# S5 tables of a hybrid diffusion step: transposing the factors of the matrix to the state, or their product

## The chip, the core and the metric

The kernel runs on one core of a Trainium2 chip. The metric is the device time of one execution in microseconds (us), the median of three runs. PE is TensorE (the matrix engine), PEld its weight loads, DVE is VectorE, ACT is ScalarE, POOL is GpSimd and SP is SyncE; the last two also issue DMAs, each on a queue of its own. Engines take their instructions in a fixed order each and wait for one another by semaphores. Lines (L138) are lines of the kernel before, except in the orders of the changed kernel, which have its own.

## The reference

One inference step of a backbone of two layers with shared weights, for 128 context tokens and 256 latent ones, of 1024 channels. A layer is a half-step SwiGLU FFN, a mixer of three branches (S5 scan, convolution, chunk MLP) and another half FFN. Only the S5 branch is touched. For each of 32 groups of 16 channels, two directions and 64 states:

```python
mag = jnp.exp(a_re * dt)
abar_r, abar_i = mag * jnp.cos(a_im * dt), mag * jnp.sin(a_im * dt)
...
bbar_r = qr[..., None] * b_re - qi[..., None] * b_im
bbar_i = qr[..., None] * b_im + qi[..., None] * b_re
bu_r = jnp.einsum('gph,blgh->blgp', bbar_r, u)
...
_, _, sr, si = lax.associative_scan(_ssm_combine, (ar, ai, bu_r, bu_i), reverse=reverse, axis=1)
y = jnp.einsum('ghp,blgp->blgh', c_re, sr) - jnp.einsum('ghp,blgp->blgh', c_im, si)
```

`abar` is the step of the state, `bbar` the factors of the input (`u` is a part of a projection), and `c` the factors of the output.

## The kernel before

**Weights.** The program is one long list of products of weights with all 384 tokens. A unit of weights (up to 512 rows by 256 columns, 128x1024 on the chip) is loaded by SP into `wr`, split by ACT into a rounded half `wh` (L126) and by DVE into the rest `wl` (L105), and used in 24 matmuls of 384 columns (L198, L199, L200, `mm3`): rounded weight by rounded input `hh` (or `ah`), by the input's rest `hl` (`al`), and rest of the weight by rounded input. `wr`, `wh` and `wl` have three buffers each, and units are asked for two ahead (`LOOK`), so the split of one waits until the matmuls of an earlier one have freed its buffers. PE's order is the one in which the code is written; the scheduler of the framework sets the order on the other engines, which follows that of writing with some interleaving.

**Tracks.** Other work is written as generators ("tracks") that go forward a little after each unit (`tick`): the modulation vectors (`modev`, L138, and `modw`, L385, on the bank `ax`) and the S5 tables (`tables`, at a rate of 1.9 steps a unit in layer 0 and 1.6 in layer 1). Where a track has PE work, this stands in PE's order between two units.

**S5 parameters.** The S5 scan is done in chunks of TC = 8 steps. `s5_params` (L776), once for both layers, works out `pw`, the powers 0 to 8 of `abar` with the state (two directions by 64) on the 128 partitions, and writes them in two orders, `w` = 0 and 1, through `px` to DRAM (`px_d`).

**S5 tables.** `s5_tables` (L912), once a layer, reads both back (`pxl`: `psx` and `pyx`) and then takes the 32 groups of channels in four "groups" of GB = 8. Each begins with two transposes of the output factors `cr` on PE into a bank `tb`, copied by ACT to `cT` (L946); the input factors `bb`, four products `cm` and two sums on DVE (L105) from `braw`; their shifted copy `bp`, four ACT copies of 64 partitions (L956, L957), both `bb` and `bp` zeroed on POOL first; and `nci` (L118). Then follow two sub-blocks of GS = 4, each with

- `my`, the matrix from the state to the outputs: powers `pyx` by `cT`, six DVE operations of 512 elements a partition, stored on POOL's queue (L993);
- `mt`, the matrix to the state: powers `psx` by `bb`, six such DVE operations (L105), with the state on the partitions;
- the responses within a chunk: 32 small matmuls of `bp`, `bb` with `my`, `cT`, `nci` (L1012, L1022), copied to `kall`;
- eight transposes of `mt` on PE (L138) into two banks, two ACT copies to `ms` (L1038), which has steps and channels on the partitions, and its store (L1039).

At the end of a group twelve small stores of `kall` to `kd` (L1042 to L1044), eight loads of `mib` (L1047), each onto 16 partitions, and the store of `mi` go by POOL's queue. In the mixer `load_to` (L1132) reads `ms` on SP's queue and PE multiplies it with `U`. Of temporaries, pool `c4` has five buffers (`my`, `mt`, `ms`, `mib`), `c2` seven (`pxl`, `bb`, `bp`, `tp`), `s1` seven (`cT`, `cm`, `braw`, `cr`, `kall`, `nci`), and of banks `tb` there are two.

Of the kernel before, what the change touches and what calls it, by code (L numbers as in the profile page):

```python
# [19 lines left out]
P = 128  # L20
DEPTH = 2
# [35 lines left out]
def hybrid_step(ctx: ExitStack, tc: tile.TileContext, I, pos_r, pos_c, y_prompt, y_sample, new_state):  # L57
# [649 lines left out]
    px_d = [drm.tile([P, 2, 2, TC, G], F32, tag=f"px{l}", name=f"px{l}") for l in range(DEPTH)]  # L707
# [68 lines left out]
    def s5_params(raw, ldt):  # L776
# [81 lines left out]
        lo_i = slice(TC - 1, None, -1), slice(1, TC + 1)  # L858
        hi_i = slice(0, TC), slice(TC, 0, -1)
        for w in range(2):  # L860
            px = c4([P, DEPTH, 2, TC, G], "px")
            for i in range(2):
                for rows, ix in ((LO, lo_i[w]), (HI, hi_i[w])):
                    src = pw[rows, i, ix, :].rearrange("p n (l g) -> p l n g", l=DEPTH)
                    for l in range(DEPTH):
                        act.activation(px[rows, l, i], src[:, l], AF.Copy)
            for l in range(DEPTH):
                q.dma_start(px_d[l][:, w], px[:, l])
# [43 lines left out]
    def s5_tables(l):  # L912
        q = nc.gpsimd
        px = []
        for w in range(2):
            t = c2([P, 2, TC, G], "pxl")
            q.dma_start(t, px_d[l][:, w])
            px.append(t)
        psx, pyx = px
# [18 lines left out]
        for gb in range(G // GB):  # L938
# [20 lines left out]
            ts_(nci, cT[:, 1], -1.0)  # L959
            if gb + 1 < G // GB:  # L960
                nxt = load_bc(gb + 1)
            kall = s1([P, 2, 9 * H], "kall")
            for sb in range(GB // GS):
                s0 = sb * GS

                def pexp(tab, i):
                    v = tab[:, i, :, g0 + s0 : g0 + s0 + GS]
                    return v.rearrange("p n g -> p g n").unsqueeze(3).to_broadcast(sh)
# [5 lines left out]
                b_r, b_i = vec(bb[:, 0]), vec(bb[:, 1])  # L974
                my = c4([P, GS, 2, TC, H], "my")
                t1, t2 = c2(sh, "tp1"), c2(sh, "tp2")
                mul(t1, pexp(pyx, 0), c_r)
                mul(t2, pexp(pyx, 1), c_i)
# [3 lines left out]
                mul(t1, pexp(pyx, 1), c_r)  # L982
                yield
                mul(t2, pexp(pyx, 0), c_i)
# [10 lines left out]
                mt = c4([P, GS, 2, TC, H], "mt")  # L995
                t1, t2 = c2(sh, "tp1"), c2(sh, "tp2")
                mul(t1, pexp(psx, 0), b_r)
                mul(t2, pexp(psx, 1), b_i)
                yield
                sub(mt[:, :, 0], t1, t2)  # L1000
                t1, t2 = c2(sh, "tp1"), c2(sh, "tp2")
# [839 lines left out]
```

## Time and profile before

| | |
|---|---|
| median of 3 runs | 1785.54 us (1782.42 to 1787.46) |
| the profiled execution | 1785.44 us, span 1783.6 us |
| busy in the span | PE 1758.1, PEld 1672.6, DVE 1247.1, ACT 795.0, POOL 202.8 us |
| tables of layer 0 | first `cr` transposes at 161.91 us, second at 207.83 us |
| DMA | 344.37 MB, mean 193 GB/s |

The profile is of one execution, by the hardware profiler. The span runs from its first instruction to its last. Register, branch, semaphore and DMA-issuing instructions are not counted as busy, matmuls overlap in time (the start of the next is the better measure of one), and a row with xN stands for N instructions in a row. "[2.37 <-DMA kd]" in a row means that the engine was idle for 2.37 us just before it and what ended that.

### The profile page before, as it was taken

What the parts mean: (1) busy time and instruction counts of PE and PEld (TensorE: products, weight loads), DVE (VectorE), ACT (ScalarE), POOL (GpSimd) and SP (SyncE); (2) the same over time, 40 slices, a digit from 0 to 9 for tenths busy, and PEclk for the clock granted to TensorE, in tenths of its full rate; (3) what the DMA queues carried; (4) which work ended last, traced back from release to release, by engine and by line L of the source; (5) the groups of instructions that cost most, each with busy time, mean ns of one, the idle gap of its engine ahead of it and who ended that gap; (6) DMA issues with size and microseconds to landing.
All of it is one profiled execution on the core that took longest, in us unless ns stands there. A gap on an engine that the chain in (4) does not pass through costs nothing.

```text
span 1783.6 us, 29079 instructions
## 1 busy us (share of the span) xinstructions
PE 1758.1 (99%) x11186; PEld 1672.6 (94%) x11186; DVE 1247.1 (70%) x2344; ACT 795.0 (45%) x1330; POOL 202.8 (11%) x400
## 2 busy tenths in 40 slices
PE   6999999999999999999999999999999999999997
PEld 4899999999999989999999899999999999999997
DVE  4496676778987776679387666777799677544435
ACT  3344333564455553233357233336744546433233
POOL 2012343310010000000001133232100000000000
PEclk9999999999999999999999999999999999999999
DMA  9768788765744567788346776667666343443332
GB/s 329 258 220 272 231 255 268 225 194 185 243 144 128 168 223 225 253 276 257 118 130 206 231 225 214 177 198 226 174 209 182 119 131 119 130 130 123 126 124 77
DMA packets 253746, 344.37 MB, mean 193 GB/s; under 512 B 22399, under 2 KB 216651, under 8 KB 253608
## 3 DMA queue, kind: packets, MB, share of 16 engines
q1 hardware_dynamic: 228504, 299.18, 52.9%
q0 software_dynamic: 17088, 39.51, 7.3%
q10 hardware_dynamic: 8016, 3.82, 0.8%
q8 instruction: 88, 1.44, 0.3%
q14 instruction: 50, 0.41, 0.1%
HBM read 309.75 MB, written 32.70 MB: 192 GB/s over the span
## 4 chain that ended last, share of the span: by engine, by line
PE 97%; DVE 1%; DMA 1%; ACT 1%; issue 0%; DVEq 0%; ACTq 0%
PE mm L198 30%; PE mm L199 29%; PE mm L200 29%; PE ax L385 3%; PE tb L1159 1%; PE tb L138 1%; PE tb L1237 1%; DMA wr<-in_w_in_dram 1%; PE tb L1012 0%; PE ax L503 0%; PE ax L138 0%; DMA crow<-in_c_dram 0%; DVE sqacc L105 0%; PE mm L1528 0%; PE ax L489 0%; PE mm L1530 0%
## 5 line engine op out<-in xcount | busy, mean ns | idle before, releaser
L105 DVE TENSOR_TENSOR wl<-wr,wh 128x1024 fp32r<-128x1024 f32 (+2 forms) x389 | 457.4, 1176 | 355.5 <-ACT wh L126 350.2
L126 ACT ACTIVATE wh<-wr 128x1024 fp32r<-128x1024 f32 (+1 forms) x387 | 395.6, 1023 | 646.4 <-PE mm L199 483.9
L198 PE MATMUL mm<-hh,wh 128*128 128x384 f32 x1840 | 628.5, 342 | 3.9 <-ACT hh L609 3.9
L199 PE MATMUL mm<-hl,wh 128*128 128x384 f32 x1840 | 616.9, 335 | 0.7 <-DVE hl L105 0.7
L200 PE MATMUL mm<-hh,wl 128*128 128x384 f32 x1840 | 616.8, 335 | 0.0
L198 PEld LDWEIGHTS mm<-hh,wh 128*128 128x128 f32 x1840 | 346.2, 188 | 33.4 <-issue 18.4
L199 PEld LDWEIGHTS mm<-hl,wh 128*128 128x128 f32 x1840 | 346.3, 188 | 1.7 <-DVE hl L105 1.5
L200 PEld LDWEIGHTS mm<-hh,wl 128*128 128x128 f32 x1840 | 346.0, 188 | 0.1
L198 PE MATMUL mm<-ah,wh 128*128 128x384 f32 x800 | 271.9, 340 | 0.0
L199 PE MATMUL mm<-al,wh 128*128 128x384 f32 x800 | 269.8, 337 | 0.0
L200 PE MATMUL mm<-ah,wl 128*128 128x384 f32 x800 | 269.4, 337 | 0.0
L198 PEld LDWEIGHTS mm<-ah,wh 128*128 128x128 f32 x800 | 150.2, 188 | 9.6 <-issue 6.7
L199 PEld LDWEIGHTS mm<-al,wh 128*128 128x128 f32 x800 | 150.3, 188 | 0.0
L200 PEld LDWEIGHTS mm<-ah,wl 128*128 128x128 f32 x800 | 150.2, 188 | 0.0
L123 DVE SCALAR_TENSOR_TENSOR x<-mm,gt,x 128x128 f32<-128x128 f32 x224 | 83.1, 411 | 33.2 <-PE mm L200 32.8
L198 PE MATMUL mm<-xh,wh 128*128 128x386 f32 x240 | 84.8, 353 | 0.0
L200 PE MATMUL mm<-xh,wl 128*128 128x386 f32 x240 | 82.0, 342 | 0.0
L199 PE MATMUL mm<-xl,wh 128*128 128x386 f32 x240 | 82.0, 342 | 0.0
L126 ACT ACTIVATE ah<-av 128x384 fp32r<-128x384 f32 x82 | 42.1, 519 | 87.8 <-DVE av L105 87.5
L123 DVE SCALAR_TENSOR_TENSOR macc<-modw,silu_c,macc 128x1024 f32<-128x1024 f32 x56 | 69.9, 1279 | 10.3 <-DMA modw<-in_w_mod_dram 10.3
L123 DVE SCALAR_TENSOR_TENSOR cacc<-pad,pv,cacc 128x399 f32<-128x399 f32 x120 | 68.6, 629 | 0.0
L385 PE MATMUL ax<-modw,silu_c 128*32 128x512 f32 (+1 forms) x576 | 62.5, 516 | 0.0
(316 smaller groups left out, 1868.0 us busy)
## 6 DMA issues: line engine op xcount, KB each, us to landing
wr<-in_ffn_w_dram SPq DMA_DIRECT2D x256, 512.0 KB, 3.6
modw<-in_w_mod_dram SPq DMA_DIRECT2D x144, 512.0 KB, 5.1
wr<-in_w_gate_dram SPq DMA_DIRECT2D x48, 512.0 KB, 4.7
wr<-in_w_in_dram SPq DMA_DIRECT2D x24, 512.0 KB, 3.9
my<-my POOLq DMA_DIRECT2D x16, 512.0 KB, 5.8
ms<-ms POOLq DMA_DIRECT2D x16, 512.0 KB, 5.2
m_ms<-ms SPq DMA_DIRECT2D x16, 512.0 KB, 5.5
m_my<-my SPq DMA_DIRECT2D x16, 512.0 KB, 9.9
```

The source lines that it names most:

```text
L105: (eng or dve).tensor_tensor(out, a, b, op=op)
L123: dve.scalar_tensor_tensor(out, a, s, b, op0=op0, op1=op1)
L126: act.activation(hi, full, AF.Copy)
L138: pe.transpose(out, in_, ident[:rows, :rows])
L198: pe.matmul(out, wh[:, k, cols], xh, start=first, stop=False)
L199: pe.matmul(out, wh[:, k, cols], xl, start=False, stop=False)
L200: pe.matmul(out, wl[:, k, cols], xh, start=False, stop=last)
L385: pe.matmul(b[32 * s : 32 * s + 32, :w], silu_c[:, k, :], raws[i][:, c : c + w], start=(k == 0), stop=(k == KD - 1), skip_group_check=True,)
L1159: pe.matmul(b[:, g * NCH : (g + 1) * NCH], d["ms"][g // GS][:, g % GS, i, :], U[:, q * GB + g, :], start=True, stop=True,)
L1237: pe.matmul(b[64 * half : 64 * half + NCH, g * P : (g + 1) * P], u, w, start=(n == 0), stop=(n == 2), skip_group_check=True,)
```

## The change

The matrix to the state is no longer formed with the state on the partitions and transposed. `s5_params` writes the powers in one order to `px_d` (half of it before), transposes `pw` itself with eight transposes, rearranges it with four ACT copies into `pws`, and writes it to DRAM (`pt_d`: real and imaginary, step, channel group, state). Each group copies its `bb` on ACT to `bc`, transposes this on PE right behind `cr`, copies the result to `bts` and writes that to DRAM (`bt_d`). For each sub-block `to_rows_in` loads both in 16 transfers of 16 partitions on POOL's queue, eight of `pt` (L1029 of the changed kernel, each powers of one step given to 16 partitions) and eight of `bt` (L1030), and `to_rows` forms `ms` by six DVE operations of 128x512, with steps and channels on the partitions. The generator of a group yields in a new order: `my` of both sub-blocks early, the second sub-block's loads behind the first one's `ms`.

```diff
-    px_d = [drm.tile([P, 2, 2, TC, G], F32, tag=f"px{l}", name=f"px{l}") for l in range(DEPTH)]
+    px_d = [drm.tile([P, 2, TC, G], F32, tag=f"px{l}", name=f"px{l}") for l in range(DEPTH)]
+    pt_d = [drm.tile([2, TC, G, P], F32, tag=f"pt{l}", name=f"pt{l}") for l in range(DEPTH)]
+    bt_d = [drm.tile([H, G, 2, P], F32, tag=f"bt{l}", name=f"bt{l}") for l in range(DEPTH)]
...
-        lo_i = slice(TC - 1, None, -1), slice(1, TC + 1)
-        hi_i = slice(0, TC), slice(TC, 0, -1)
-        for w in range(2):
-            px = c4([P, DEPTH, 2, TC, G], "px")
-            for i in range(2):
-                for rows, ix in ((LO, lo_i[w]), (HI, hi_i[w])):
-                    src = pw[rows, i, ix, :].rearrange("p n (l g) -> p l n g", l=DEPTH)
-                    for l in range(DEPTH):
-                        act.activation(px[rows, l, i], src[:, l], AF.Copy)
+        px = c4([P, DEPTH, 2, TC, G], "px")
+        for i in range(2):
+            for rows, ix in ((LO, slice(1, TC + 1)), (HI, slice(TC, 0, -1))):
+                src = pw[rows, i, ix, :].rearrange("p n (l g) -> p l n g", l=DEPTH)
+                for l in range(DEPTH):
+                    act.activation(px[rows, l, i], src[:, l], AF.Copy)
+        for l in range(DEPTH):
+            q.dma_start(px_d[l], px[:, l])
+        yield
+
+        pws = c4([P, TC, P], "pws")
+        for i in range(2):
+            b = tb_bank()
+            for m in range(TC // 2):
+                transpose(
+                    b[:, m * P : (m + 1) * P], pw[:, i, 2 * m : 2 * m + 2, :].rearrange("p n r -> p (n r)"), P
+                )
+            bv = b.rearrange("p (m s) -> p m s", s=P)
+            o = pws[:, 4 * i : 4 * i + 4]
+            act.activation(o[:, ::-1, LO], bv[:, :, LO], AF.Copy)
+            act.activation(o[:, :, HI], bv[:, :, HI], AF.Copy)
+            yield
+        for n2 in range(2):
             for l in range(DEPTH):
-                q.dma_start(px_d[l][:, w], px[:, l])
+                r = n2 * NG + l * G
+                rows_d = pt_d[l].rearrange("i j g s -> (i j) g s")
+                for half, off in ((LO, 1 - n2), (HI, n2)):
+                    q.dma_start(
+                        rows_d[off::2, :, half].rearrange("m g s -> g m s"), pws[r : r + G, :, half]
+                    )
...
-        px = []
-        for w in range(2):
-            t = c2([P, 2, TC, G], "pxl")
-            q.dma_start(t, px_d[l][:, w])
-            px.append(t)
-        psx, pyx = px
+        pyx = c2([P, 2, TC, G], "pxl")
+        q.dma_start(pyx, px_d[l])
...
             nci = s1([P, GB, H], "nci")
             ts_(nci, cT[:, 1], -1.0)
+            bc = s1([P, 2, GB, H], "bc")
+            act.activation(bc, bb[:, :, :, :H], AF.Copy)
+            b = tb_bank()
+            for i in range(2):
+                transpose(b[:, i * P : (i + 1) * P], bc[:, i].rearrange("p g h -> p (g h)"), P)
+            bts = s1([P, 2, P], "bts")
+            act.activation(bts.rearrange("p i s -> p (i s)"), b[:, : 2 * P], AF.Copy)
+            q.dma_start(bt_d[l][:, gs].rearrange("h g i s -> g h (i s)"), bts.rearrange("r i s -> r (i s)"))
             if gb + 1 < G // GB:
                 nxt = load_bc(gb + 1)
             kall = s1([P, 2, 9 * H], "kall")
-            for sb in range(GB // GS):
+
+            def from_rows(sb):
...
-                mt = c4([P, GS, 2, TC, H], "mt")
-                t1, t2 = c2(sh, "tp1"), c2(sh, "tp2")
-                mul(t1, pexp(psx, 0), b_r)
-                mul(t2, pexp(psx, 1), b_i)
+
+            def to_rows_in(sb):
+                gr = slice(g0 + sb * GS, g0 + (sb + 1) * GS)
+                pt = c4([P, 2, GS, P], "pt")
+                bt = c4([P, GS, 2, P], "bt")
+                for j in range(TC):
+                    rows = slice(j * H, (j + 1) * H)
+                    src = pt_d[l][:, j, gr]
+                    q.dma_start(pt[rows], src.unsqueeze(0).to_broadcast([H, 2, GS, P]))
+                    q.dma_start(bt[rows], bt_d[l][:, gr])
+                ins.append((pt, bt))
+
+            def to_rows(sb):
+                pt, bt = ins[sb]
+                ms = c4([P, GS, 2, P], "ms")
+                t1, t2 = (c2([P, GS, P], f"tp{i}") for i in (1, 2))
+                mul(t1, pt[:, 0], bt[:, :, 0])
+                mul(t2, pt[:, 1], bt[:, :, 1])
                 yield
-                sub(mt[:, :, 0], t1, t2)
-                t1, t2 = c2(sh, "tp1"), c2(sh, "tp2")
-                mul(t1, pexp(psx, 0), b_i)
+                sub(ms[:, :, 0], t1, t2)
+                t1, t2 = (c2([P, GS, P], f"tp{i}") for i in (1, 2))
+                mul(t1, pt[:, 0], bt[:, :, 1])
                 yield
-                mul(t2, pexp(psx, 1), b_r)
-                add(mt[:, :, 1], t1, t2)
-                for _ in range(3):
-                    yield
+                mul(t2, pt[:, 1], bt[:, :, 0])
+                add(ms[:, :, 1], t1, t2)
+                q.dma_start(ms_d[l][:, g0 + sb * GS : g0 + (sb + 1) * GS], ms)
+                yield
+
+            def responses(sb):
+                s0 = sb * GS
+                my = mys[sb]
                 b = tb_bank()
 
                 for i in range(2):
@@ -1028,15 +1072,19 @@
                             skip_group_check=True,
                         )
                 act.activation(kall[:, sb, :], b[:, : 9 * H], AF.Copy)
-                ms = c4([P, GS, 2, P], "ms")
-                for g2 in range(0, GS, 2):
-                    b = tb_bank()
-                    for j in range(4):
-                        transpose(
-                            b[:, j * P : (j + 1) * P], mt[:, g2 + j // 2, j % 2].rearrange("p i h -> p (i h)"), P
-                        )
-                    act.activation(ms[:, g2 : g2 + 2].rearrange("p g r c -> p (g r c)"), b, AF.Copy)
-                q.dma_start(ms_d[l][:, g0 + s0 : g0 + s0 + GS], ms)
+
+            mys, ins = [], []
+            yield from from_rows(0)
+            to_rows_in(0)
+            yield from from_rows(1)
+            responses(0)
+            yield from to_rows(0)
+            to_rows_in(1)
+            yield
+            yield
+            responses(1)
+            yield
+            yield from to_rows(1)
```

What this does to the orders, at the last change of group in layer 0 (from the third to the fourth group).

PE, at the transposes of `cr` between two units of the first FFN or the mixer, before (`hh`, `hl` the inputs of the matmuls, `tb` a bank):

```order
L198 MATMUL mm<-hh_527,wh 128x384
L199 MATMUL mm<-hl_528,wh 128x384
L200 MATMUL mm<-hh_527,wl 128x384
L138 MATMUL tb<-ident,cr 128x128 x2
L198 MATMUL mm<-hh_345,wh 128x384
L199 MATMUL mm<-hl_346,wh 128x384
L200 MATMUL mm<-hh_345,wl 128x384
```

and in the changed kernel:

```order
L198 MATMUL mm<-hh_531,wh 128x384
L199 MATMUL mm<-hl_532,wh 128x384
L200 MATMUL mm<-hh_531,wl 128x384
L138 MATMUL tb<-ident,cr 128x128 x2
L138 MATMUL tb<-ident,bc 128x128 x2
L198 MATMUL mm<-hh_349,wh 128x384
L199 MATMUL mm<-hl_350,wh 128x384
```

The two transposes of `bc` stand directly behind those of `cr`, with no matmul of weights between them.

DVE, before, at the input factors `bb` of the fourth group (`cm` are the products, `wl` splits of weights):

```order
L105 TENSOR_TENSOR al<-av,ah 128x384
L105 TENSOR_TENSOR wl<-wr,wh 128x1024
L105 TENSOR_TENSOR cm_3360<-q_t,braw 128x128
L105 TENSOR_TENSOR cm_3361<-q_t,braw 128x128
L105 TENSOR_TENSOR cm_3365<-q_t,braw 128x128
L105 TENSOR_TENSOR bb<-cm_3360,cm_3361 128x8x16
L105 TENSOR_TENSOR cm_3366<-q_t,braw 128x128
L105 TENSOR_TENSOR wl<-wr,wh 128x1024
L105 TENSOR_TENSOR bb<-cm_3365,cm_3366 128x8x16
L118 TENSOR_SCALAR nci<-cT 128x128
L105 TENSOR_TENSOR tp_3380<-pxl,cT 128x512
L105 TENSOR_TENSOR tp_3381<-pxl,cT 128x512
```

and in the changed kernel, the operations just ahead of the same two sums `bb` (`tp`, `ms` are of the third group, both sub-blocks):

```order
L105 TENSOR_TENSOR tp_3159<-pt,bt 128x512
L105 TENSOR_TENSOR ms<-tp_3154,tp_3155 128x4x128
L105 TENSOR_TENSOR tp_3160<-pt,bt 128x512
L105 TENSOR_TENSOR ms<-tp_3159,tp_3160 128x4x128
L105 TENSOR_TENSOR tp_3306<-pt,bt 128x512
L105 TENSOR_TENSOR tp_3307<-pt,bt 128x512
L105 TENSOR_TENSOR tp_3311<-pt,bt 128x512
L105 TENSOR_TENSOR ms<-tp_3306,tp_3307 128x4x128
L105 TENSOR_TENSOR tp_3312<-pt,bt 128x512
L105 TENSOR_TENSOR ms<-tp_3311,tp_3312 128x4x128
L105 TENSOR_TENSOR bb<-cm_3428,cm_3429 128x8x16
L105 TENSOR_TENSOR bb<-cm_3433,cm_3434 128x8x16
```

The sums `bb` stand behind the twelve operations on `pt` and `bt` of the group in hand, and behind `nci` of the fourth group there is no weight split between them.

POOL, in the changed kernel, around the store of the first `ms` of the third group (`kd` are the small stores of `kall`):

```order
L1019 DMA my_130<-my 128x1024
L1090 DMA kd_132<-kall 16x2x112
L1091 DMA kd_132<-kall 16x2x112
L1092 DMA kd_132<-kall 16x2x16
L1090 DMA kd_132<-kall 16x2x112
L1029 DMA pt<-pt_142 16x2x512
L1046 DMA ms_128<-ms 128x1024
L1030 DMA bt<-bt_144 16x1024
L1029 DMA pt<-pt_142 16x2x512
L1030 DMA bt<-bt_144 16x1024
L1029 DMA pt<-pt_142 16x2x512
L1030 DMA bt<-bt_144 16x1024
```

One load of `pt` of the second sub-block stands ahead of the store of `ms`, and fifteen of the sixteen behind it.

## Rows read from the trace of the kernel before

**Rows 1.** The page, busy times (part 1) and the chain (part 4).

```profile
PE 1758.1 (99%) x11186; PEld 1672.6 (94%) x11186; DVE 1247.1 (70%) x2344; ACT 795.0 (45%) x1330; POOL 202.8 (11%) x400
...
PE 97%; DVE 1%; DMA 1%; ACT 1%; issue 0%; DVEq 0%; ACTq 0%
```

**Rows 2.** What PE waited for (us in total, times, longest): first and last of eight.

```profile
PE ax L138 <- DMA crow<-in_c_dram: 5.9, 1, 5.9
...
PE ax L138 <- ACT pv L322: 0.4, 1, 0.4
```

**Rows 3.** Busy time by stretch; after the stretch: its us, engines, PEclk, DMA share, GB/s.

```profile
163.00:211.00 48.00, 48.00 (x343) 43.28 (x343) 33.91 (x55) 19.68 (x35) 10.74 (x21) 1.00 0.72 238
211.00:256.00 45.00, 45.00 (x327) 41.52 (x327) 34.08 (x61) 16.16 (x25) 21.38 (x41) 1.00 0.83 245
```

**Rows 4.** Timeline of PE, end of a sub-block (start us, us, engine, line, operation).

```profile
182.03 1.24 PE L138 MATMUL tb<-ident,mt 128*128 128x128 f32 x8
183.03 0.42 PE L198 MATMUL mm<-hh,wh 128*128 128x384 f32 x1
```

**Rows 5.** Timeline of all engines at the first group of layer 0.

```profile
161.56 0.33 PE L199 MATMUL mm<-hl,wh 128*128 128x384 f32 x1
...
161.91 0.38 PE L138 MATMUL tb<-ident,cr 128*128 128x128 f32 x2
...
162.05 0.42 PE L198 MATMUL mm<-hh,wh 128*128 128x384 f32 x1
...
162.90 0.37 ACT L946 ACTIVATE cT<-tb 128x256 f32<-128x256 f32 x1
...
163.44 0.28 DVE L105 TENSOR_TENSOR bb<-cm,cm 128x128 f32<-128x128 f32 x1
...
164.11 0.31 ACT L957 ACTIVATE bp<-bb 64x128 f32<-64x128 f32 x1
```

**Rows 6.** Timeline of DVE, operations of the tables.

```profile
175.08 1.29 DVE L105 TENSOR_TENSOR tp<-pxl,bb 128x512 f32<-128x512 f32 x2
...
178.17 0.68 DVE L105 TENSOR_TENSOR mt<-tp,tp 128x512 f32<-128x512 f32 x1
```

**Rows 7.** The tile mib: its loads (ns minimum/median/maximum), and their landing.

```profile
L1047 POOL DMA_DIRECT2D mib<-kd x64: 528/528/545, 217.3 to 1219.3; - x64
...
DMA to landing us min/median/max: 2.6/5.8/8.8
```

**Rows 8.** Timeline of POOL, the small stores of kall.

```profile
210.18 0.50 POOL L1043 DMA_DIRECT2D kd<-kall  x1 [2.37 <-DMA kd<-kall]
...
212.59 0.50 POOL L1042 DMA_DIRECT2D kd<-kall  x1 [1.42 <-DMA ms<-ms]
```

**Rows 9.** Groups of instructions, shapes apart (busy us, mean ns, idle before): the weight splits.

```profile
L105 DVE TENSOR_TENSOR wl<-wr,wh 128x1024 fp32r<-128x1024 f32 x355 | 434.0, 1223 | 326.8 <-ACT wh L126 321.6 <-PE ax L385 3.5
L126 ACT ACTIVATE wh<-wr 128x1024 fp32r<-128x1024 f32 x355 | 375.4, 1058 | 583.8 <-PE mm L199 455.7 <-issue 113.8 <-DMA wr<-in_ffn_w_dram 6.2
```

**Rows 10.** Timeline of PE at the third group of layer 0.

```profile
249.57 0.34 PE L200 MATMUL mm<-ah,wl 128*128 128x384 f32 x1
...
251.32 0.60 PE L138 MATMUL ax<-ident,modev 128*128 128x128 f32 x4
251.85 1.06 PE L385 MATMUL ax<-modw,silu_c 128*32 128x512 f32 x8
252.85 0.44 PE L138 MATMUL tb<-ident,cr 128*128 128x128 f32 x2
```

**Rows 11.** Busy time by stretch, as rows 3, near the program's start.

```profile
16.00:20.00 4.00, 3.13 (x26) 1.64 (x26) 1.30 (x5) 0.78 (x3) 0.00 (x0) 0.95 1.06 365
20.00:24.00 4.00, 2.98 (x20) 0.80 (x18) 2.32 (x9) 1.33 (x2) 0.00 (x0) 0.62 1.08 365
24.00:28.00 4.00, 2.14 (x7) 1.85 (x7) 3.96 (x11) 1.31 (x3) 0.00 (x0) 0.81 1.05 385
28.00:32.00 4.00, 4.00 (x23) 3.12 (x22) 3.49 (x8) 1.73 (x3) 0.00 (x0) 0.77 1.05 387
```

More of the change, by code (lines that the diff above doesn't have):

```diff
@@ L962, in s5_tables, with pexp @@
             kall = s1([P, 2, 9 * H], "kall")
-            for sb in range(GB // GS):
+            def from_rows(sb):
                 s0 = sb * GS
-                def pexp(tab, i):
-                    v = tab[:, i, :, g0 + s0 : g0 + s0 + GS]
+                def pexp(i):
+                    v = pyx[:, i, :, g0 + s0 : g0 + s0 + GS]
                     return v.rearrange("p n g -> p g n").unsqueeze(3).to_broadcast(sh)
@@ L973, in s5_tables @@
                 c_r, c_i = vec(cT[:, 0]), vec(cT[:, 1])
-                b_r, b_i = vec(bb[:, 0]), vec(bb[:, 1])
                 my = c4([P, GS, 2, TC, H], "my")
+                mys.append(my)
                 t1, t2 = c2(sh, "tp1"), c2(sh, "tp2")
-                mul(t1, pexp(pyx, 0), c_r)
-                mul(t2, pexp(pyx, 1), c_i)
+                mul(t1, pexp(0), c_r)
+                mul(t2, pexp(1), c_i)
                 yield
@@ L981, in s5_tables @@
                 t1, t2 = c2(sh, "tp1"), c2(sh, "tp2")
-                mul(t1, pexp(pyx, 1), c_r)
+                mul(t1, pexp(1), c_r)
                 yield
-                mul(t2, pexp(pyx, 0), c_i)
+                mul(t2, pexp(0), c_i)
                 stt(
```

## The prediction

> **What bounds the kernel now.** I read the page's busy times first, then the chain that ended last, then what the PE (the matrix engine) waited for, and only then the stretches of the S5 tables. The PE is busy for 1758.1 us of the span of 1783.6 us, and 97% of the last chain is PE time [rows 1]. Its waits are few: eight kinds, the longest 5.9 us, the last 0.4 us [rows 2]. So whatever is taken off the PE's list shortens the kernel, and whatever makes the PE stand lengthens it by as much. DVE, ACT and POOL have room: in the table stretches DVE works 34 of 48 us and 34 of 45 us, while the PE works all of them [rows 3]. The execution that is profiled took 1785.44 us, 0.1 us from the median of the runs; the sum is made against it.
>
> **What is removed.** In each of 16 sub-blocks (eight per layer) eight transposes of `mt` end a burst of small matmuls. They run from 182.03 us to the next weight matmul at 183.03 us: 1.00 us [rows 4]. 16 x 1.00 = 16.0 us off the PE. The two ACT copies behind them go too, beside an idle ACT: nothing.
>
> **What is added on the PE.** Eight transposes of the powers, once, at an eighth of that microsecond each: 1.0 us. Two transposes of `bc` per group of eight channels, eight pairs. The pair for `cr`, of the same shape, starts at 161.91 us, the next matmul at 162.05 us, and that one lasts 0.42 us instead of 0.33 us: 0.23 us a pair, 1.8 us in all [rows 5]. Net work on the PE: -16.0 + 1.0 + 1.8 = **-13 us**.
>
> **What is moved.** The six DVE operations of the matrix to the state remain six of 512 elements a partition; two of them start 0.605 us apart (1.29 us for two that last 0.68 us) [rows 6]. So DVE's sum is unchanged. But their inputs are now loaded: 16 transfers of 64 KB a sub-block on POOL's queue, 256 in all. The nearest row is the eight `mib` loads, also 64 KB onto 16 partitions: 0.528 us of POOL each, and 2.6 to 8.8 us to landing, 5.8 us at the median [rows 7]. POOL also stops when its eighth-last transfer has not landed: 2.37 us and 1.42 us in one run of small transfers [rows 8]. 256 x 0.528 = 135 us of POOL, which is busy for only 202.8 us [rows 1]: no cost by itself.
>
> **The added wait.** The transposes of `bc` stand on the PE directly behind those of `cr`, with no weight matmul between, and wait for ACT's copy of `bb`, which waits for DVE. In the DVE order of the change, `bb` of the next group stands behind all twelve operations of the group in hand, the second six of which wait for loads. I walk the last change of group in layer 0, counted from the PE's arrival.
>
> 1. The last weight split ahead needs the buffer of the unit the PE has just finished: ACT 1.058 us, DVE 1.223 us [rows 9]; with `nci` 2.5 us. Then six operations of the first half, 3.6 us: they end at 6.1 us.
> 2. Only now can POOL store the first `ms`, and behind it stand fifteen of the sixteen loads of the second half. 15 x 0.528 = 7.9 us to the last start. For a landing I take 5.0 us, a little under the median, because the weight loads stop while the PE stands. The ninth transfer then waits 5.5 - 4.2 = 1.3 us for the first. With 0.5 us to issue and 5.0 us to land, all is there 14.7 us after point 1, at 20.8 us.
> 3. Six operations 3.65 us, two of `bb` 0.4 us, four copies of `bp` at 0.31 us (ACT is in order and they stand ahead), the copy `bc` at `cT`'s 0.37 us [rows 5], hand-overs 0.2 us: 5.9 us.
>
> The PE stands 6.1 + 20.6 = 26.7 us. The other changes differ in when the first half ends. Layer 0, first change: the split ahead of it is freed two units earlier, 2 x 4.2 us (24 matmuls 0.175 us apart, [rows 10]): it ends at about -2 us. Layer 0, second: work on `modev` and `modw` stands before `cr`; the rows before show 251.32 to 252.85 us, 1.5 us [rows 10], and a wait for ACT's copy is near it now: 3.5 us. Layer 1, second and third: 2 us and 5 us. Layer 1, first: the half ends some 11 us early and the walk gives 10 us, but `bb` is first zeroed on POOL behind loads and small stores; I take 14 us. The first group of each layer has no predecessor. In the rows before, `bb` is done at 163.72 us, `bp` at 164.42 us, `bc` would be at 164.8 us, and the PE is past `cr` at 162.1 us: 2.7 us in layer 1 [rows 5]; in layer 0 a weight split stands ahead now: 4.4 us.
>
> Layer 0: 4.4 + 18.6 + 24.1 + 26.7 = 73.8 us. Layer 1: 2.7 + 14 + 22.6 + 25.6 = 64.9 us. **Together +139 us.** Queued behind `bb` on DVE are six to ten table operations and then weight splits; two or three units are already split, some 8 us of PE work, so I add nothing. U and the other POOL loads of the mixer move with the PE: nothing.
>
> **The clock.** Between 16 and 32 us the PE had little to do in three of four windows (2.14 to 3.13 of 4 us busy) and its granted clock averaged 0.95, 0.62, 0.81, 0.77, a mixture of 2.4 and 1.2 GHz: 4 x 0.85 = 3.4 us lost [rows 11]. I charge half of that to each of the six long stands: **+10 us**; the low bound is nothing. The Trainium skill, page "TensorE: Matmul & The Clock Gate", Part 1, says that the throttled state is the default and activity releases it; by that rule every long stand is followed by slow matmuls, which the trace agrees with at the 0.62 after a thin stretch.
>
> The Trainium skill, page "DMA: Bandwidth & Descriptors", Anatomy of one DMA (GpSimd path), fits 2.0 us plus bytes over 436 GB/s per transfer, 2.15 us for 64 KB, against the 5.8 us of the rows; an estimate by that page would put the kernel near 1900 us.
>
> **Sum.** 1785.4 - 13 + 139 + 10 = **1921 us**.
>
> **Bounds.** With the shortest landing of the rows, 2.6 us, there is no wait for the ninth transfer and each of five changes is 3.7 us shorter, 1901 us; without the clock 1891 us; with first halves 3 us earlier, 1875 us. With the longest, 8.8 us, the later transfers slip by 5.1 us and land 3.8 us later, minus the 1.3 us already counted: 7.6 us more for each of five, 38 us; layer 1's first change about 8 us; and the first halves, fed by such loads too, up to 5 us later: 1921 + 38 + 8 + 25 = 1992 us.
>
> **Rivals.**
> - *Loads are there in time.* If POOL had issued the second half's loads before the PE arrives, a change would cost the split 2.5 us, up to 7.3 us of operations, and 2.3 us for `bb` and copies: 8 to 12 us, some 10. 6 x 10 + 7 - 13 = +54 us, about 1840 us. Against it: the first `ms` stands in POOL's queue ahead of fourteen or fifteen of those loads in five of the six changes. Chance 0.08.
> - *Faster.* The place is the eight pairs of `bc`. If `bc` is ready whenever the PE gets there, only the -13 us is left: 1772 us. It decides at zero wait, that is `bb` written some 2 us before `cr`. For it: DVE idles in these stretches. Against it: even the rows before, with nothing ahead of `bb`, have it 1.6 us after `cr`. Chance 0.02.
> - *No change to measure.* Stands of 13 us in all would cancel the gain; the two first groups alone bring 7 us. Chance 0.01. That the transposes do not go at all is excluded by the PE's order, where `mt` no longer stands.
> - *POOL becomes the bound.* Landings of 9 us and more with eight in flight: a group then needs more POOL time than its nine units of PE work give, and the backlog grows from group to group. Above 1995 us. For it: the table stretches already have a DMA share of 0.72 and 0.83 [rows 3]. Against it: the weight loads pause in each stand. Chance 0.08.
>
> The forecast has 0.81. The range, 1865 to 1995 us, leaves out the two rivals at its ends and a little of the forecast. About 0.3% (5 us) is what can be told from no change here. Faster 0.02, same 0.01, slower 0.97.
>
> **What would show it.** In the profile after, the PE's waits should be led by the transposes on `tb` waiting for ACT's `bc` copy, eight times, two short (3 to 5 us) and six of 14 to 27 us; DVE should wait for `pt` or `bt` loads ahead of its second half; POOL should carry 256 more transfers; and the granted clock should dip behind the stands. I am wrong if those eight waits are below 60 us together, or if the PE instead starves for weights or for the mixer's U.

## The result

The changed kernel takes 1938.52 us (median of four runs, 1936.95 to 1940.89) against 1786.5 us of the kernel before: a ratio of 1.0854, 95% interval 1.084 to 1.0867. The forecast was 1921 us in a range of 1865 to 1995 us, and slower.

The page of the changed kernel, part 1, which answers to [rows 1]:

```profile
PE 1773.5 (92%) x11082; PEld 1684.5 (87%) x11082; DVE 1248.2 (64%) x2344; ACT 783.6 (40%) x1310; POOL 339.8 (18%) x668
```

The span is 1936.8 us, 153.2 us longer. The PE's busy time grew by 15.4 us; the other 137.8 us are time in which it stood. What it waited for (us in total, times, longest), to be read beside [rows 2]:

```profile
PE tb L138 <- ACT bc L978: 124.5, 8, 23.4
PE ax L138 <- ACT modev L395: 6.3, 3, 4.4
...
PE ax L489 <- DVE sqacc L105: 4.7, 2, 3.2
PE mm L198 <- DVE xh L524: 4.2, 2, 3.2
```

The first row is the one that was looked for: eight waits of the `bc` transposes for ACT's copy, 124.5 us. The other waits grew by 13.3 us. The eight, from the PE's timeline, with the stand in brackets:

```profile
173.08 0.69 PE L138 MATMUL tb<-ident,bc 128*128 128x128 f32 x2 [3.51 <-ACT bc L978]
...
236.41 0.69 PE L138 MATMUL tb<-ident,bc 128*128 128x128 f32 x2 [16.98 <-ACT bc L978]
...
299.74 0.69 PE L138 MATMUL tb<-ident,bc 128*128 128x128 f32 x2 [20.21 <-ACT bc L978]
...
368.81 0.69 PE L138 MATMUL tb<-ident,bc 128*128 128x128 f32 x2 [22.86 <-ACT bc L978]
...
1093.14 0.44 PE L138 MATMUL tb<-ident,bc 128*128 128x128 f32 x2 [3.21 <-ACT bc L978]
...
1157.84 0.69 PE L138 MATMUL tb<-ident,bc 128*128 128x128 f32 x2 [13.23 <-ACT bc L978]
...
1228.29 0.69 PE L138 MATMUL tb<-ident,bc 128*128 128x128 f32 x2 [21.12 <-ACT bc L978]
...
1301.20 0.69 PE L138 MATMUL tb<-ident,bc 128*128 128x128 f32 x2 [23.36 <-ACT bc L978]
```

The walk had 4.4, 18.6, 24.1 and 26.7 us for layer 0 and 2.7, 14, 22.6 and 25.6 us for layer 1. The order of size is right in each layer, and each long stand is 0.8 to 3.9 us shorter than forecast. The first halves ended nearly when the walk had them end, counted from the arrival: at -3.5, 2.4 and 5.9 us in layer 0 (forecast -2, 3.5 and 6.1) and at -12.1, 1.7 and 4.6 us in layer 1 (forecast -11, 2 and 5). At the first change of layer 1 all loads had been issued before the arrival. There DVE waited 2.30 us for one of them and then 1.36 us for POOL to zero `bb`, behind loads and small stores, as the prediction had it.

The fourth of them in detail. The PE arrives at 368.81 - 22.86 = 345.95 us. DVE:

```profile
346.74 1.23 DVE L105 TENSOR_TENSOR wl<-wr,wh 128x1024 fp32r<-128x1024 f32 x1 [0.45 <-ACT wh L126]
...
348.01 1.89 DVE L105 TENSOR_TENSOR tp<-pt,bt 128x512 f32<-128x512 f32 x3
...
351.14 0.69 DVE L105 TENSOR_TENSOR ms<-tp,tp 128x512 f32<-128x512 f32 x1
362.93 1.89 DVE L105 TENSOR_TENSOR tp<-pt,bt 128x512 f32<-128x512 f32 x3 [11.10 <-DMA kd<-kall]
...
366.06 0.69 DVE L105 TENSOR_TENSOR ms<-tp,tp 128x512 f32<-128x512 f32 x1
366.67 0.48 DVE L105 TENSOR_TENSOR bb<-cm,cm 128x128 f32<-128x128 f32 x2
```

The split (`wl`) comes first, then the six operations of the first half, which end at 351.83 us, 5.9 us after the arrival. DVE then waits 11.10 us for the second half's loads. (The row names a `kd` store, the last transfer of POOL's queue that the wait covers; the loads are seen on POOL.) POOL:

```profile
352.13 0.59 POOL L1046 DMA_DIRECT2D ms<-ms  x1 [17.07 <-DVE ms L105]
352.71 0.52 POOL L1030 DMA_DIRECT2D bt<-bt  x1
...
359.71 0.49 POOL L1030 DMA_DIRECT2D bt<-bt  x1
```

The store of the first `ms` waited 17.07 us for DVE, and only behind it the fifteen loads go out, one each half microsecond, the last at 359.71 us. It has landed by 362.93 us. Then six operations, `bb`, and on ACT the copies of `bp` ahead of `bc`:

```profile
367.05 0.31 ACT L973 ACTIVATE bp<-bb 64x128 f32<-64x128 f32 x1 [19.70 <-DVE bb L105]
...
368.34 0.42 ACT L978 ACTIVATE bc<-bb 128x256 f32<-128x256 f32 x1
```

That is the walk, point by point. What the stand does to the clock (columns as in [rows 3]; the granted clock is the third figure from the end):

```profile
346.00:368.70 22.70, 0.00 (x0) 0.00 (x0) 11.08 (x20) 2.95 (x8) 14.69 (x29) 0.58 0.45 122
369.00:373.00 4.00, 4.00 (x14) 4.00 (x14) 4.00 (x7) 0.38 (x1) 1.44 (x3) 0.50 0.38 102
373.00:377.00 4.00, 4.00 (x24) 2.91 (x23) 0.51 (x2) 1.06 (x1) 2.88 (x6) 0.91 0.52 130
377.00:381.00 4.00, 4.00 (x25) 4.00 (x24) 2.02 (x3) 0.55 (x2) 4.00 (x8) 1.00 1.00 249
```

While the PE stands it is granted 0.58 on average, 0.50 at the end, and the first 4 us of work run at 0.50, that is 1.2 GHz; from 377 us it is at 1.00 again. The Trainium skill, page "TensorE: Matmul & The Clock Gate", Part 1, has the low state as the default and activity as what ends it; these rows agree. Over windows of 4 us from 40 us on, busy time by the missing share of the clock sums to 27.5 us, against 1.8 us in the kernel before.

### The profile page after: what moved, and what is told of

It is laid out like the page before. It is cut to its first block, busy times and chain, and to the rows that moved or that the text cites. A ratio compares the mean times of both kernels' runs of the same rounds, so it can differ in the third digit from the quotient of the medians.

```text
span 1936.8 us, 29152 instructions
## 1 busy us (share of the span) xinstructions
PE 1773.5 (92%) x11082; PEld 1684.5 (87%) x11082; DVE 1248.2 (64%) x2344; ACT 783.6 (40%) x1310; POOL 339.8 (18%) x668
## 5 line engine op out<-in xcount | busy, mean ns | idle before, releaser
L198 PEld LDWEIGHTS mm<-hh,wh 128*128 128x128 f32 x1840 | 350.6, 191 | 35.8 <-issue 19.3
L199 PEld LDWEIGHTS mm<-hl,wh 128*128 128x128 f32 x1840 | 350.4, 190 | 1.6 <-DVE hl L105 1.2
L200 PEld LDWEIGHTS mm<-hh,wl 128*128 128x128 f32 x1840 | 350.2, 190 | 0.1
L138 PE MATMUL tb<-ident,bc 128*128 128x128 f32 x16 | 5.3, 429 | 124.5 <-ACT bc L978 124.5
L105 DVE TENSOR_TENSOR tp<-pt,bt 128x512 f32<-128x512 f32 x64 | 41.2, 685 | 66.6 <-DMA kd<-kall 64.1
```

What stands on the lines that cost most here:

```text
L105: (eng or dve).tensor_tensor(out, a, b, op=op)
L138: pe.transpose(out, in_, ident[:rows, :rows])
L198: pe.matmul(out, wh[:, k, cols], xh, start=first, stop=False)
L199: pe.matmul(out, wh[:, k, cols], xl, start=False, stop=False)
L200: pe.matmul(out, wl[:, k, cols], xh, start=False, stop=last)
```

## The experiments

All times are medians beside runs of the kernel before on the same chip (1784.6 to 1787.52 us).

| run | what is changed | us | ratio, 95% interval |
|---|---|---|---|
| e1 | before, `bc` added | 1824.87 | 1.0222 (1.0201 to 1.0243) |
| e2 | before, transposes taken out | 1773.84 | 0.9939 (0.9924 to 0.9953) |
| e3 | change, loads in the modulation's buffers | 1994.68 | 1.1172 (1.1147 to 1.1197) |
| e4 | change, `bb` a group ahead | 1915.1 | 1.0727 (1.0707 to 1.0747) |
| e5 | change, loads in own buffers | 1925.92 | 1.0776 (1.0741 to 1.0811) |
| e6 | e5, loads written first | 1894.61 | 1.0596 (1.0565 to 1.0626) |
| e7 | e6 with e4 | 1881.07 | 1.0531 (1.0494 to 1.0568) |
| e8 | e7, few large loads | 1851.64 | 1.0352 (1.0321 to 1.0383) |
| e9 | e7, zeroing and `braw` off POOL | 1859.79 | 1.0407 (1.0386 to 1.0428) |
| e10 | e8, zeroing and `braw` off POOL | 1794.0 | 1.0051 (1.003 to 1.0073) |
| e11 | e10, powers spread by group | 1805.97 | 1.0107 (1.0085 to 1.0129) |
| e12 | e11, responses later | 1806.37 | 1.012 (1.0103 to 1.0137) |

**e1: the place behind `cr` by itself.**

```diff
             ts_(nci, cT[:, 1], -1.0)
+            bc = s1([P, 2, GB, H], "bc")
+            act.activation(bc, bb[:, :, :, :H], AF.Copy)
+            b = tb_bank()
+            for i in range(2):
+                transpose(b[:, i * P : (i + 1) * P], bc[:, i].rearrange("p g h -> p (g h)"), P)
+            bts = s1([P, 2, P], "bts")
+            act.activation(bts.rearrange("p i s -> p (i s)"), b[:, : 2 * P], AF.Copy)
```

> The kernel before, with one part of the change added: the ACT copy bc, its two transposes directly behind those of cr and the copy bts (nothing reads bts; no loads, and mt is still transposed). Theory 'order' (the long stands come from bb being queued on DVE behind operations that wait for loads; the place behind cr alone costs only the copies): in the rows before, the last bp copy ends 2.4 to 3.2 us after the PE has passed cr, so with bc the eight waits should be 2.9 to 3.6 us, some 26 us together; the transposes 1.8 us; and behind each short stand 1.4 to 2.9 us at the low clock, as behind the two short stands of the changed kernel (11 to 23 us). Together 39 to 51 us over before, about 1830 us. If short stands cost no clock: 1814 us. Rival 'place' (the position directly behind cr is what costs, whatever stands ahead of bb): most of the 152 us, above 1900 us.

It took 38.9 us more than before, at the low end of the 39 to 51 us expected. What the PE waited for:

```profile
PE tb L138 <- ACT bc L961: 23.2, 8, 3.2
```

Eight waits of 2.60 to 3.21 us, a little under the 2.9 to 3.6 us worked out from the rows of before, so the place alone explains 23 of the 124.5 us; the rival "place" falls. The low clock, summed as above, is 14.9 us, 13.1 more than before; 12.1 us of it lie behind these stands. It is not the same behind each: the two of 2.61 and 2.65 us had none, the others some 1.5 to 3.1 us each.

**e2: the transposes by themselves.** `mt` is stored as `ms` without being turned; this leaves the turning out and is for the time alone.

```diff
-                ms = c4([P, GS, 2, P], "ms")
-                for g2 in range(0, GS, 2):
...
-                q.dma_start(ms_d[l][:, g0 + s0 : g0 + s0 + GS], ms)
+                q.dma_start(ms_d[l][:, g0 + s0 : g0 + s0 + GS], mt.rearrange("p g r i h -> p g r (i h)"))
```

> The kernel before without the 128 transposes of mt and the 32 copies behind them; mt is stored as ms as it stands, so the matrix to the state is not turned. This is the term '-16.0 us' of the sum by itself. If the PE's list is the bound there: 16 us less than before, 1770 us. Rival (the transposes fill time in which the PE would wait anyway): within 5 us of before.

```profile
PE 1745.7 (98%) x11058; PEld 1661.3 (94%) x11058; DVE 1246.3 (70%) x2344; ACT 776.9 (44%) x1298; POOL 201.8 (11%) x400
```

12.1 us less by the medians, and 12.4 us less of PE time (1758.1 to 1745.7). The transposes were on the path. What a burst takes of the PE's list is seen at the end of a sub-block, before and then in e2 (what follows it before is in [rows 4]):

```profile
181.87 0.23 PE L1022 MATMUL tb<-nci,bb 128*32 128x16 f32 x8
```

```profile
182.96 0.23 PE L1022 MATMUL tb<-nci,bb 128*32 128x16 f32 x8
183.13 0.45 PE L198 MATMUL mm<-hh,wh 128*128 128x384 f32 x1
```

From the matmuls with `nci` to the next weight matmul it is 1.16 us before and 0.17 us in e2, so 0.99 us go with the burst. Over all sixteen bursts, with the first weight matmul behind each, it is 15.6 us. The time fell by 3.5 us less than that. In the profiled execution, the longest of the four (1776.69 us), the PE is idle for 29.2 us instead of 25.5 us, with a new wait of 2.2 us for `al` and 1.7 us more for `sqacc`; whether these waits are in the others too is not shown.

**e3 and e5: is it the order on POOL, or the buffers?** In the change `pt` and `bt` take two of the five buffers of `c4`, and the second `bt` needs the first one's. Both runs move them elsewhere.

```diff
-                pt = c4([P, 2, GS, P], "pt")
-                bt = c4([P, GS, 2, P], "bt")
+                pt = m6([P, 2, GS, P], "pt")
+                bt = m6([P, GS, 2, P], "bt")
```

> The changed kernel with pt and bt in buffers of the mixer's pool m6 (four, free during the FFN) instead of c4, and nothing else: the second sub-block's loads no longer need a buffer that the first one's operations free; on POOL's queue 12 of its 16 loads still stand behind the store of the first ms, before 15. Theory 'order' (POOL's queue holds the loads back, not the buffers): the long stands are about 3 x 0.5 us shorter each, 1938 - 9 = about 1929 us (1918 to 1938). Rival 'buffers' (bt's second tile waits for the first one's buffer): the loads are there when the PE arrives, six stands of 8 to 12 us instead of 13 to 23, about 60 us less, and the 13 us of other waits go too: about 1865 us.

```profile
PE ax L385 <- DMA modw<-in_w_mod_dram: 84.7, 15, 11.7
PE tb L138 <- ACT bc L978: 78.8, 8, 16.1
```

Neither theory had 1995 us. The pool `m6` is also that of the modulation's weights, `modw`, which now came late. The run says nothing clean, so e5 repeats it in `c3`:

> As e3 (pt and bt out of c4, the rest of the changed kernel as it is), but in the pool c3, which no weights of the modulation use; its tiles grow to 4 KB and the temporaries t go from eight buffers to seven to make room. In e3 the waits for bc fell from 124.5 to 78.8 us, while 84.7 us of waits for modw came up, whose buffers pt and bt had taken. Theory 'buffers' (half of the wait for the second loads was bt's buffer): the waits for modw go, those for bc stay near 79 us, with the low clock 25 us and 10 us of other waits: 1786 - 13 + 79 + 25 + 10 = about 1887 us (1865 to 1905). Theory 'order' as first stated (POOL's queue alone): the waits for bc come back above 110 us, 1920 us or more.

```profile
PE tb L138 <- ACT bc L978: 119.8, 8, 24.6
```

The waits for `bc` are back at 119.8 us. DVE's waits for the loads did fall, from 66.4 to 45.3 us, and the second group of each layer now stands 10.5 instead of 17.0 and 13.2 us; but the third and fourth stand as long as in the change (20.8 to 24.6 us), with twelve or thirteen loads behind the `ms` store on POOL. So the buffers explain a little in two places, and POOL's order is enough for the rest. Why e3's waits for `bc` were so short was not traced; a PE that stands for `modw` gives the loads time, but that is only argued.

**e4: only `bb` ahead.** The four products and two sums of the next group's `bb`, and `bc`, stand behind the first `my`, their transposes and store behind the first responses. The pool `c2` has eight buffers here.

```diff
             yield from from_rows(0)
+            if gb + 1 < G // GB:
+                nbb = inputs(gb + 1, nxt[0])
...
             responses(0)
+            if gb + 1 < G // GB:
+                turn(gb + 1, nbb[1])
             yield from to_rows(0)
```

> The changed kernel with bb and bc of a group formed, transposed and written one group earlier (bb behind the first my of the group before, the transposes behind that group's first responses); the loads stay as they are. Theory 'order': the waits of the PE for bc vanish (below 3 us together), and so does the low clock behind them. DVE still waits some 11 us a group for loads, with weight splits queued behind; two units, 8 us of PE work, are split ahead, so the PE sees 0 to 4 us of each: 1786 - 13 + 8 x 3 = about 1797 us (1775 to 1820). Rival 'loads' (what costs is that DVE waits for transfers, wherever bb stands): the stands move to the weight halves wh and wl, and the time stays above 1880 us.

```profile
PE tb L1070 <- DVE my L105: 42.1, 5, 14.4
PE tb L138 <- ACT bc L959: 35.5, 4, 11.1
PE ax L138 <- ACT modev L395: 18.1, 5, 8.4
```

The theory was wrong by 118 us here: four waits for `bc` are left, and the time is above the 1880 us of the rival "loads". The stands did not move to `wh` and `wl`, as that rival had it (2.8 and 4.3 us). The PE stands at the next thing that DVE owes it, mostly `my` for the responses. DVE still waits 30.1 us for loads of `pt` and `bt` and 24.6 us for those of `braw`, and what is behind them in its list is late, so the place of `bb` alone decides little more than which wait gets the blame: 23 us.

**e6 and e7: the loads early.** The loads of both halves are written at the head of a group; e7 has e4's `bb` as well.

```diff
             mys, ins = [], []
+            to_rows_in(0)
+            to_rows_in(1)
             yield from from_rows(0)
-            to_rows_in(0)
...
             yield from to_rows(0)
-            to_rows_in(1)
```

> As e5, and all 32 loads of a group are written right behind the store of bt, ahead of everything else of the group; bb stays behind the table operations on DVE. Theory 'order and loads' (a stand is the DVE work ahead of bb, and the loads' lateness on top): no wait for loads is left, so six stands of some 10 us (a split 2.5, up to twelve operations 7.3, bb and copies 2.3), 7 us for the first two: 67 us of waits for bc, clock 20 us: 1786 - 13 + 67 + 20 = about 1860 us (1835 to 1880). If POOL's queue is too slow for 33 transfers a group whatever the place they are written at: no faster than e5.

> As e6, and bb, bc, their transposes and store are one group ahead as in e4. e4 moved the stand from bc to my and to the modulation, since DVE was still held by loads. If lateness of loads and the place of bb are all there is: 1786 - 13 + 0 to 12 = 1773 to 1785 us. If POOL's queue holds loads back (in its order they stand behind the twelve small stores of the group before): DVE waits for loads still, 1800 to 1850 us.

e6 is 31 us faster than e5, but the stands are still 96.4 us, 29 more than its theory, about what DVE now waits for POOL. Of the PE, and then of DVE:

```profile
PE tb L138 <- ACT bc L978: 96.4, 8, 17.2
```

```profile
DVE bb L105 <- POOL bb L965: 30.0, 6, 5.8
```

DVE no longer waits for a load of `pt` or `bt`. It waits for POOL to zero `bb`, and in e7 for 62.2 us in all. One such wait, on POOL and on DVE:

```profile
240.83 0.53 POOL L1043 DMA_DIRECT2D pt<-pt  x1
...
260.94 0.49 POOL L1044 DMA_DIRECT2D bt<-bt  x1
...
261.99 0.54 POOL L953 MEMSET bb<- 128x512 f32 x1
```

```profile
262.57 0.29 DVE L105 TENSOR_TENSOR bb<-cm,cm 128x128 f32<-128x128 f32 x1 [16.40 <-POOL bb L953]
```

The zeroing stands behind 24 of the group's 32 loads, which were issued from 240.83 to 261.43 us; eight follow it. Some 12 us of this are the issues, and 8.3 us are stops of POOL for transfers that had not landed. POOL's one list carries stores, loads and zeroing, and the 33 transfers a group had pushed `bb` back another way.

**e8: fewer transfers.** Powers and input factors are written to DRAM once for each of the 128 rows; a sub-block then takes two loads.

```diff
-                for j in range(TC):
...
+                q.dma_start(pt, pr_d[l][:, :, :, gr].rearrange("j h i g s -> (j h) i (g s)"))
+                q.dma_start(bt, bt_d[l][:, :, gr].rearrange("j h g i s -> (j h) (g i s)"))
```

> As e7, but powers and input factors stand in DRAM once for each of the 128 rows: the powers are spread by 16 transfers from DRAM to DRAM once, the input factors by eight stores a group, and a sub-block then takes 2 loads of 512 KB instead of 16 of 64 KB. POOL issues 12 transfers a group for them instead of 33. If POOL's queue was what held e7 back: 1773 to 1785 us, and faster than before by up to 13 us. If it is the bytes: slower than e7, since 8 MB more are written.

```profile
PE tb L138 <- ACT bc L969: 43.3, 7, 13.1
PE mm L198 <- ACT wh L126: 10.4, 1, 10.4
```

```profile
DVE cm L105 <- DMA braw<-in_s_b_re_dram: 34.2, 6, 10.5
```

29 us better than e7, and short of its goal for two reasons: `braw`, loaded by POOL behind all else, was late for DVE by 34.2 us, and the PE stood once for 10.4 us for a weight half while the powers were being spread.

**e9 and e10: the zeroing and `braw` off POOL.** The loads of `cr` go to SP's queue too.

```diff
-            pool.memset(bb, 0.0)
+            dve.memset(bb[:, :, :, H:], 0.0)
...
-                    q.dma_start(braw[d * PS : (d + 1) * PS, i], I[nm][l, d, gs].rearrange("g p h -> p g h"))
+                    nc.sync.dma_start(braw[d * PS : (d + 1) * PS, i], I[nm][l, d, gs].rearrange("g p h -> p g h"))
```

> As e7, with the zeroing of bb and bp moved from POOL to DVE (only the halves that stay zero) and the loads of braw and cr moved from POOL's queue to SP's. In e7 DVE waited 62.2 us for POOL's zeroing of bb, which stood behind the 32 loads, and the PE 90.9 us for bc. Theory 'queue' (what holds bb back now is POOL's order of work, no longer its own place on DVE): the waits for bc fall below 20 us, with 8 us of low clock and 10 us of other waits 1786 - 13 + 20 + 8 + 10 = about 1810 us (1785 to 1825). Rival 'transfers' (33 small transfers a group land too late for DVE whatever stands beside them): DVE waits for loads of pt and bt, and the time stays above 1840 us.

```profile
PE tb L1071 <- DVE my L105: 43.0, 4, 14.8
PE ax L138 <- ACT modev L395: 12.2, 4, 6.3
PE tb L138 <- ACT bc L959: 7.0, 3, 4.0
```

The waits for `bc` fell from 90.9 to 7.0 us, as the theory "queue" had it, but 43.0 us for `my` and 12.2 us for the modulation took their place; 1860 us is the rival's side. DVE's waits for loads of `pt` and `bt` are not among its rows, though, so the rival's mechanism is not shown either: ahead of the longest `my` waits stand the table operations of the group before and, in two of three, a wait of 3.97 or 4.66 us for a transfer ahead of `cm`.

> As e8 (powers and input factors spread in DRAM, 2 loads of 512 KB a sub-block), with the zeroing on DVE and braw and cr on SP's queue as in e9, and the spreading of the powers given out over the steps of the rotations instead of in one go (in e8 the PE waited 10.4 us for weights beside it). In e8 DVE waited 34 us for braw and the PE 43.3 us for bc. Theory 'queue': waits for bc below 10 us, 1773 to 1795 us. Rival 'bytes' (16 MB more of traffic delay the weights): above 1800 us with waits of the PE for wh or of ACT for wr.

```profile
PE tb L1079 <- DVE my L105: 8.1, 1, 8.1
...
PE tb L138 <- ACT bc L961: 1.6, 1, 1.6
```

With few transfers as well, nearly all is gone: 1794.0 us, inside the expected range, and 144 us of the change's loss recovered. The powers are also spread step by step here, so the 58 us over e8 are not the cleared list's alone. It is still 0.3 to 0.7% slower than before: the PE is busy for 1752.7 us, 5.4 us less than before, but idle for 13.9 us more. ACT's waits for `wr`, which the rival "bytes" had named, are there (73.5 us in all, 10.5 us before), but the PE waited only 1.1 us for `wh`. Its waits for `my` and `bc` lie in the first group of layer 0, from 198 to 203 us. Ahead of them ACT waited for weights, which were being loaded while the powers were spread, and DVE for `braw`:

```profile
164.30 1.06 ACT L126 ACTIVATE wh<-wr 128x1024 fp32r<-128x1024 f32 x1 [9.40 <-DMA wr<-in_ffn_w_dram]
```

```profile
187.31 0.29 DVE L105 TENSOR_TENSOR cm<-q_t,braw 128x128 f32<-128x128 f32 x1 [7.64 <-DMA braw<-in_s_b_re_dram]
```

**e11 and e12: after the rest.** e11 spreads the powers a group at a time and forms the next `bb` behind the first responses; e12 puts two idle steps ahead of the first responses.

```diff
+            yield
+            yield
             responses(0)
...
-            yield
-            yield
             responses(1)
```

> As e10, but the powers are spread in DRAM group by group, two transfers of 2 MB in all a group ahead (in e10 eight of 512 KB went out at once near 142 us, ACT then waited 9.4 and 4.2 us for weights), and the next group's bb is formed behind the first responses instead of behind the first my (in e10 DVE waited 7.6 us for braw of the second group, and the PE 8.1 us for my behind it). e10's waits that the kernel before does not have are some 11 us, with 3 to 4 us of low clock. Theory (nothing else was wrong in e10): 1794 - 14 = about 1780 us (1774 to 1787), a little faster than before. Rival (the extra traffic costs in other places): 1790 us or more.

```profile
PE tb L1086 <- DVE my L105: 13.0, 4, 4.8
```

> As e11, with the first responses of a group two steps later in the PE's order (the two idle steps ahead of the second responses stand ahead of the first now, so a group is no longer). In e11 six waits of the PE for my, 2 to 5 us each and 15.1 us together, took the place of e10's, since DVE had my late by that much. Theory (the PE only comes too early for my by some 5 us, about one unit of weights): these waits go and the low clock behind them, some 9 us by 6 x 1.5; 1806 - 15 - 9 = about 1782 us (1774 to 1790). Rival (DVE is simply behind, and another wait takes its place, or the added traffic costs): 1795 us or more.

```profile
PE tb L1086 <- DVE my L105: 10.9, 4, 3.3
```

Both lost 12 us against e10, and the time is on the rival's side in each. In e11 the PE is idle for 7.7 us more than in e10 and busy for 4.8 us more, with 6.6 us more of the low clock. The burst of the powers no longer holds weights, but now every group of layer 0 waits 2 to 5 us for `my`. Moving the responses back by about a unit did not help: in the order that the scheduler then made for DVE, one more weight split stands ahead of the first `my`. Whether another order would bring the -12 us of e2 to the end is open. No version beat the kernel before.

## Why the prediction was right

- **What is removed, -16.0 us: right as work of the PE.** The sixteen bursts took 15.6 us of its list; in time e2 gives -12.1 us.
- **What is added on the PE, 2.8 us: about right.** In the changed kernel the eight transposes of the powers take 0.79 us from the first to the next matmul, and in e1 a pair for `bc` takes 0.19 us in the five faster cases of eight: 2.3 us in all.
- **The added wait, +139 us: right in kind and place, 14.5 us too large.** 124.5 us, in the order that the walk gave. In the fourth stand the first half ended 5.9 us after the arrival (6.1 forecast) and the tail from the last landing to the start of the transposes took 5.9 us (5.9 forecast). The step that was mis-sized is point 2: I let the ninth transfer wait 1.3 us for the first and gave 5.5 us to issue and land; the fifteen loads went out without a break, and the last had landed 3.2 us after its start. Together that is 3.6 of the 3.8 us by which this stand is shorter. In the other four changes with late loads POOL did stop between them, for 0.9 to 2.7 us, and the last load had landed 2.9 to 3.1 us after its start in three of them and 5.2 us in one. So it is the landing that was too long: loads of `pt` and `bt` that started while the PE stood for `bc` landed in 3.9 us at the median (66 loads, 2.5 to 7.2 us), the others in 6.1 us (190 loads), near the 5.8 us of [rows 7]. The median of all was the wrong row for a queue that has a standing PE beside it. The Trainium skill, page "DMA: Bandwidth & Descriptors", Anatomy of one DMA — SWDGE (gpsimd) path, would have 2.15 us for such a load, an estimate from its fit; none of the 256 landed as fast (2.5 us the least).
- **The clock, +10 us: too small.** The low clock costs 27.5 us, 25.7 more than before. Of the 27.5 us, 14.5 lie behind the six long stands (2.4 each; I had charged 1.7), 4.3 behind the two short ones, for which I had charged nothing, and 7.2 at the ends of the tables, behind waits I had not forecast, below. The 1.7 was half of what I took for a thin stretch; counted by busy time, as here, that stretch of [rows 11] lost 2.6 us, and a stand loses about all of that. Another 1.6 us are not the change's: they follow a stand of 1.93 us near 44 us that the kernel before has too, there without a loss.
- **"I add nothing" for what is queued behind `bb` on DVE: wrong.** The other waits of the PE grew by 13.3 us. The largest are at the end of layer 0's tables, where the last group has no `bc` behind it but DVE still waits for loads. DVE, and then the PE:

```profile
437.36 1.89 DVE L105 TENSOR_TENSOR tp<-pt,bt 128x512 f32<-128x512 f32 x3 [11.29 <-DMA kd<-kall]
```

```profile
441.91 0.62 PE L198 MATMUL mm<-xh,wh 128*128 128x386 f32 x1 [3.19 <-DVE xh L524]
...
447.97 1.44 PE L489 MATMUL ax<-ones,sqacc 128*128 128x1 f32 x6 [3.25 <-DVE sqacc L105]
```

  The inputs `xh` of the next stage and the sums `sqacc` stand behind those operations; the PE stood 3.19 and 3.25 us (2.19 for `sqacc` before). A wait of 4.37 us for `modev`, at 426.02 us, is one of ACT's order: its copy starts 13.4 us behind the matmuls of `modw`, after splits and squares, and 1.1 us behind them before.
- **The sum.** -15.6 + 2.3 + 124.5 + 13.3 + 25.7 = 150.2 us, against 153.2 us of span; 3 us stay unexplained. That the forecast came within 18 us is in part luck: the stands were 14.5 us too long, the clock and the other waits 29 us too short. The low bounds were added up wrongly, too: five changes shorter by 3.7 us each give 1902.5, 1892.5 and 1877.5 us, not 1901, 1891 and 1875.
- **The rivals.** "Loads are there in time" was priced at 1840 us; e6, which takes the late loads away, gives 1895 us, because POOL's list then delays `bb` by the zeroing (30.0 us) and the low clock, which that price left out, costs 19 us more than before. "POOL becomes the bound" did not happen in the change, but POOL's list stands behind the waits that are left in e7 (zeroing) and e8 (`braw`). "Faster" at -13 us has its ceiling measured by e2, and e10 comes within 22 us of it.
- **What would show it:** eight waits for `bc`, two of them short and six of 13.2 to 23.4 us, DVE's waits ahead of the second half in all six, POOL busy for 339.8 instead of 202.8 us (+137; 135 forecast) and the dips of the clock are all there.

## What to carry to other kernels

Work taken off the bound engine is only worth its price if nothing that this engine waits for in order has been moved behind a transfer; before counting the gain, walk each in-order list (here DVE, then POOL) from the wait back to what is issued last. An engine that also issues DMAs has one list for all it does: behind 24 small loads a zeroing of half a microsecond kept DVE waiting 16 us. Fewer, larger transfers and a cleared list together recovered 144 of 152 us, either of the two alone 79 to 87 us (e9, e8). And when one wait is removed, look which consumer of the same late engine comes next: e4 and e9 moved the stand rather than ended it.

## What the runs showed of the hardware that I had not expected

- Stands as short as 2.6 to 3.2 us already bring the PE down to 1.2 GHz in six cases of eight (e1), for some 1.5 to 3.1 us of lost work; in two, of 2.61 and 2.65 us, the granted clock stayed at 1.00. The length of a stand does not settle it: a stand of 2.60 us lost 1.7 us, and one of 1.93 us near 45 us, which the kernel before, the changed one and e1 all have, lost 1.6 us in the changed kernel, 1.2 us in e1 and nothing in the kernel before.
- Loads of 64 KB onto 16 partitions landed in 3.9 us at the median when they started while the PE stood, and in 6.1 us otherwise; the last of the fourth stand had landed 3.2 us after its start.
- Copies from DRAM to DRAM, eight of 512 KB issued within 5 us, held the weight loads beside them so long that ACT stood 9.40 us for one (e10). In e11, which spreads them by group, its longest such wait between 100 and 450 us is 2.8 us.
